# Longer operand tiles: four buffers of a tag begin at four different places of a 128-byte line

## The chip, the cores and the metric

The kernel runs on one NeuronCore of a Trainium2 chip. The metric is the device time of one execution in microseconds (us); the median of several runs counts. TensorE, VectorE (DVE), ScalarE (ACT), GpSimd (POOL) and SyncE (SP) run their own queues and meet at semaphores. SBUF has 128 partitions; a tile occupies the same bytes of every partition.

## The reference

Two decoder layers over 256 tokens of 2048 features, all in float32:

```
x += NSA(rmsnorm(x));       x += square(relu(rmsnorm(x) @ w_up)) @ w_down     (layer 0)
k, v = rmsnorm(x) @ w_kv                                                      (shared, once)
x += DiffAttn(rmsnorm(x));  x += square(relu(rmsnorm(x) @ w_up)) @ w_down     (layer 1)
return rmsnorm(x)
```

NSA has 16 query heads and 4 key heads of 128. It has three branches: keys and values compressed from blocks of 32 tokens by a small MLP, selected blocks, and a window. With 256 tokens all blocks are selected and the window covers everything. DiffAttn takes the difference of two softmaxes for each of 16 heads. The hidden width of the MLPs is 8192, so the four MLP weights are most of the 390 MB that are read.

## The kernel before, in words

**Split products.** TensorE multiplies a reduced form of float32 (fp32r). To keep the precision, each operand is split into a high part (`split`, L144: a copy on ScalarE that rounds) and a low part (a subtraction on VectorE), and a product is three matmuls: high by high, high by low, low by high (`mm3`, L139). All of these are issued at L132.

**The weight stream.** `plan` lists 368 units of 512 x 512 weights in the order of use. `issue_raw` (L253) loads a unit as two halves into `raw` tiles, `issue_split` (L265) splits each half into a tile `wh` and a tile `wl` of 128 x 1024. Loads run up to four units ahead of use, splits two. Each of the tags `raw`, `wh`, `wl` has four buffers, so that two units of split weights are on the chip.

**The products.** There are three kinds, by what is stationary in the array and what streams through it (the moving operand):
- `unit_mm` (L291) in `proj` and `out_proj`: stationary are 128 x 128 pieces of activations in a `big` tile, moving are 512 columns of `wh` or `wl`. One unit is 24 matmuls, 12 on each half.
- `unit_mm` in the MLP's down projections: the same, but the activations lie in a `kv` tile.
- `up_unit` (L704): the weights are stationary (128 columns of `wh` or `wl`), the activations in `big` are moving: 512 columns (high and low parts side by side) with `wh`, then 256 columns (high part) with `wl`, in turn. One unit is 16 pairs.

The MLP goes through four groups (G) of 2048 hidden units: four chunks of up projections (64 pairs each), then 16 units of down projections. In the compression (`cmp_units`, L506) the stationary operand is `X[j][:, l, :]`, 120 columns or 480 bytes for each l, in a `big` tile; moving are `wh` and `wl`.

**The order.** TensorE's order is written out: the stream of units runs on, and generators for the attention heads, transposes and so on are resumed between its steps (`tick`, L107). The queues of TensorE and SyncE keep this order; the other engines' instructions are ordered by the framework.

**Where tiles lie.** `T` (L70) takes a tile of a tag from the pool; a tag has a fixed number of buffers (`BUFS`, L66), which its tiles take in turn. The tags lie one behind the other in each partition, the buffers of a tag one behind the other. A buffer of `big` has 16384 bytes, of `wh` and `wl` 4096, of `kv` 8192; these are multiples of 128, so all four buffers of a tag begin at the same place within 128 bytes. From the sizes of all that lies before them, `big` begins 64 bytes past a multiple of 128, and `wh`, `wl` and `kv` 96. The query tiles `qth` and `qtl` begin at 96 too.

Of the kernel before, what the change touches and what calls it, by code (L numbers as in the profile page):

```python
# [20 lines left out]
EPS = 1e-6  # L21
NEG = -3.0e38
FLOOR = -1.0e38
# NSA heads: waits before the scores, the transposes and the values; head to head; first head
WAIT_A = (2.0, 12.5, 4.0, 1.5, 7.0)
# differential heads: the same, and before the normed output's transposes
WAIT_B = (1.0, 8.5, 5.0, 5.5, 9.0, 7.0)
LAMBDA_INIT = 0.8 - 0.6 * math.exp(-0.3 * 1)

# [2 lines left out]
def kernel(  # L32
# [24 lines left out]
    sb = ctx.enter_context(tc.tile_pool(name="sb", bufs=2))  # L57
# [4 lines left out]
    def name(s):  # L62
        uid[0] += 1
        return f"{s}_{uid[0]}"

    BUFS = dict(raw=4, wh=4, wl=4, big=4, kv=4, q=3, qth=2, qtl=2, sa=2, sbt=2,  # L66
                psh=1, psl=1, pwh=1, pwl=1,
                ss=2, rs=2, rb=1, nrs=1, mx=3, den=3, sq=2)

    def T(shape, tag, dt=F32):  # L70
        return sb.tile(shape, dt, tag=tag, name=name(tag), bufs=BUFS[tag])

    PB = dict(acc=4, tp=4)

    def PT(tag):
        return pp.tile([P, 512], F32, tag=tag, name=name(tag), bufs=PB[tag])

# [1 line left out]
    # The weight products run as a steady stream; the pieces that wait on other  # L79
    # engines are generators, resumed between the stream's steps once the time  # L80
    # that they asked for has gone by on the tensor engine's own count.
    clock = [0.0]
    tasks = []
    seq = [0]
# [22 lines left out]
    def tick():  # L107
        if tasks and tasks[0][0] <= clock[0]:
            step()
# [21 lines left out]
    def mm(o, l, r, start, stop, shared=False):  # L131
        nc.tensor.matmul(o, lhsT=l, rhs=r, start=start, stop=stop, skip_group_check=shared)  # L132
        clock[0] += max(o.shape[-1], 256) / 2400.0

    def transpose(o, i, idn):
        nc.tensor.transpose(o, i, idn)  # L136
        clock[0] += 0.11
# [6 lines left out]
    def split(h, l, src, scale=None):  # L144
        if scale is None:
            nc.scalar.activation(h, src, AF.Copy)  # L146
            nc.vector.tensor_tensor(l, src, h.bitcast(F32), ALU.subtract)  # L147
        else:
            nc.scalar.activation(h, src, AF.Copy, scale=scale)
            nc.vector.scalar_tensor_tensor(l, src, scale, h.bitcast(F32), ALU.mult, ALU.subtract)  # L150

    ctx.enter_context(tc.manual_schedule(engines={mybir.EngineType.PE, mybir.EngineType.SP}))

# [1 line left out]
    cst = cp.tile([P, 640], F32, name="cst")  # L155
    ident = cst[:, 0:128]
    cmask = cst[:, 128:384]
# [20 lines left out]
    gates = cp.tile([P, 2, 48], F32, name="gates")  # L178
# [14 lines left out]
    def g_kv(k):  # L193
        return gcol2[:, 32 + k:33 + k]

# [1 line left out]
    plan = []  # L197

    def add_units(w, rows, c0):
# [12 lines left out]
        add_units(win, range(4), c * 512)  # L212

    def out_order():
        # (column chunk, head group): the later a group's heads come out, the later its part
        return ([(0, 0), (1, 0), (0, 1), (1, 1), (2, 0), (2, 1), (3, 0), (3, 1)] + [(2, 2), (3, 2), (0, 2), (1, 2)]
                + [(c, 3) for c in range(4)])

# [3 lines left out]
    for c, g in out_order():  # L222
        add_units(nsa_w_out[0], [g], c * 512)

    def down_order(last):
        # (column chunk, quarter of the group's rows); at the very end the last quarters of two
        # chunks stay on chip and are used for one token tile after the other
        if not last:
            return [(c, u) for c in range(4) for u in range(4)]
        return ([(c, u) for c in range(2) for u in range(4)] + [(c, u) for c in (2, 3) for u in range(3)]  # L230
                + [(2, 3), (3, 3)])
# [13 lines left out]
    for c, g in out_order():  # L245
        add_units(diff_w_out[0], [g], c * 512)
# [3 lines left out]
    units = {}  # L250
# [47 lines left out]
                    start and kk == 0, stop and kk == 3)  # L298
                tick()

# [1 line left out]
    def new_stats():  # L302
        return T([P, 2, 4], "ss"), T([P, 2], "rs")

# [28 lines left out]
                          tp[:, kk * 256:(kk + 1) * 256], gf(k))  # L333

    def new_xt():
        # two tiles of eight feature blocks: [feature, block, part, token]
        return [T([P, 8, 2, S], "big", F32R) for _ in range(2)]

    def rope(dst, src, n, rot, ct, stb):
# [17 lines left out]
        return o  # L357

    def transpose_k(src, th, tl):
        # th, tl: [dk, kv head, token block, token]  # L360
        for pr in range(2):
            if pr:
                yield 0.8
            tp = PT("tp")
            for hh in range(2):
                for t in range(2):
                    h = pr * 2 + hh
                    transpose(tp[:, hh * 256 + t * P:hh * 256 + (t + 1) * P],
                              src[:, t, h * P:(h + 1) * P], ident)
            hs = slice(2 * pr, 2 * pr + 2)  # L370
            split(th[:, hs], tl[:, hs], tp.rearrange("p (h t q) -> p h t q", h=2, t=2))
# [5 lines left out]
    def new_kv(*shape):  # L377
        return T([P, *shape], "kv", F32R)


# [1 line left out]
    with tc.high_priority():  # L382
        for c in range(4):
            if c == 0:
# [16 lines left out]
        nc.vector.tensor_scalar(gsub, gcol2[:, 48:49], 1.0 - LAMBDA_INIT, None, ALU.mult)  # L401
        yield 0.0

    # =========================== layer 0: NSA ===========================
    ss, rs = new_stats()
    xt = new_xt()
    xts = [spawn(xt_chunk(c, [(lambda k: g_attn(0, k), xt)]), 5.5 * c - 2.0) for c in range(4)]
# [58 lines left out]
        X.append(T([P, 32, 120], "big", F32R))  # L466
        tX.append(spawn(make_X(tok, X[j], j)))

    # gates: the stationary operand holds both parts of the weights side by side
    gwp = [T([P, 8, 96], tag, F32R) for tag in ("wh", "wl")]  # L470
    for i in range(2):
        split(gwp[i][:, :, 0:48], gwp[i][:, :, 48:96], gw[:, 8 * i:8 * i + 8, :])
# [89 lines left out]
    half = cp.tile([P, 1], F32, name="half")  # L562
# [139 lines left out]
        return done  # L702

    def up_unit(us, ps, xt, k0):  # L704
        # weights stationary: the product comes out with the hidden units on partitions, the
        # part with the high half of the activations and the one with the low half side by side
        for pair in range(2):
            for kk in range(4):
                wh, wl = us[kk // 2]
                k = k0 + kk  # L710
                both = xt[k // 8][:, k % 8].rearrange("p s q -> p (s q)")
                for b in (2 * pair, 2 * pair + 1):
                    bs = slice(b * P, (b + 1) * P)
                    mm(ps[b], wh[:, kk % 2, bs], both, k == 0, False)
                    mm(ps[b][:, 0:S], wl[:, kk % 2, bs], both[:, 0:S], False, k == 15)
                tick()
# [75 lines left out]
    mlp(0, mxt, rs2, hook0, done)  # L792
    finish_stats(ssd, rsd)

    # =========================== layer 1: differential attention ===========================
    lamt = T([P, 256], "sbt")
    nc.gpsimd.dma_start(lamt, diff_lambda.rearrange("b f d -> b (f d)").to_broadcast([P, 256]))
    lv = lamt.rearrange("p (a b d) -> p a b d", a=2, b=2)
# [10 lines left out]
    ps = proj(kxt, before=xts)  # L809
    t_ = evac_tok(ps, rsd)  # L810
    rope(t_, t_, 8, 16, cosB, sinB)
    # keys of the two components side by side, each with zeros on the other's rows:
    # [.., kv head, (first tile: c0, c1; second tile: c0, c1), key]
    dkh, dkl, dv = new_kv(4, 4, P), new_kv(4, 4, P), new_kv(2, 4, 2, P)
    for d in (dkh, dkl):
        for cc in range(2):
# [19 lines left out]
    ready = [spawn(diff_keys(), 6.0)]  # L836
    ps = proj(kxt)
    for t in range(2):
        # [key, key tile, kv head, part, value column]
        split(dv[:, t, :, 0, :], dv[:, t, :, 1, :], ps[t].rearrange("p (g d) -> p g d", g=4), rsd[:, t:t + 1])  # L840

    oth, otl = T([P, 16, 256], "big", F32R), T([P, 16, 256], "big", F32R)
# [2 lines left out]
    def diff_head(hd, qr):  # L845
        g, i = hd // 4, hd % 4
# [44 lines left out]
        yield WAIT_B[2]  # L891
        yield from s_o.take()
        o = PT("tp")
        # columns: (first tile: main, low part of the values; second tile: the same)
        for t, blocks in ((0, ((0, 0),)), (1, ((1, 0), (2, 1)))):
            for n, (s_, kt) in enumerate(blocks):
                a = slice(s_ * P, (s_ + 1) * P)
# [68 lines left out]


def _consts():
    """Identity, causal masks and rotary tables: they depend on the shapes alone."""
    import numpy as np  # L970

    c = np.zeros((128, 640), np.float32)
    p = np.arange(128)
    c[:, 0:128] = np.eye(128, dtype=np.float32)
    c[:, 256:384] = np.where(p[None, :] <= p[:, None], 0.0, NEG)
    n = np.arange(32)
    for t in range(2):
        ok = (n[None, :] < 15) & (16 * n[None, :] + 31 <= (t * 128 + p)[:, None])
        c[:, 384 + 32 * t:416 + 32 * t] = np.where(ok, 0.0, NEG)

    def tables(head_dim, o):
        rot = head_dim // 4
        h = rot // 2
        e = (np.arange(0, rot, 2, dtype=np.float32) / np.float32(rot)).astype(np.float32)
        inv = (np.float32(1.0) / np.power(np.float32(500000.0), e)).astype(np.float32)
        ang = np.arange(S, dtype=np.float32)[:, None] * inv[None, :]
        cos, sin = np.cos(ang).astype(np.float32), np.sin(ang).astype(np.float32)
        for t in range(2):
            r = slice(t * 128, (t + 1) * 128)
            c[:, o + t * rot:o + t * rot + h] = cos[r]  # L990
            c[:, o + t * rot + h:o + (t + 1) * rot] = cos[r]
            b = o + 2 * rot + t * rot
            c[:, b:b + h] = -sin[r]
            c[:, b + h:b + rot] = sin[r]

    tables(128, 448)
    tables(64, 576)
    return c
# [24 lines left out]
```

## Time and profile before

| | |
|---|---|
| median of 3 runs | 2161.58 us (2161.39 to 2163.61) |
| profiled execution: span from its first to its last instruction | 2159.3 us |
| profiled execution: its own time | not recorded apart from the span; the median of the runs is 2.3 us above the span |
| mean granted TensorE clock | 0.999 |
| read from HBM | 390.47 MB, 182 GB/s over the span |

[...] What a matmul costs the stream is the time from its start to the start of the next, and that is got from a stretch's length and its count of matmuls.

### The profile page before, as it was taken

The page shows a single profiled execution, that of the slowest core. Times are in us where ns is not written, and L with a number is a line of the kernel's source. Part 1 is how long each engine was busy: PE and PEld are TensorE (multiplying, and loading weights), DVE is VectorE, ACT ScalarE, POOL GpSimd, SP SyncE. Part 2 cuts the span into 40 slices and gives each one's busy share as a digit, 9 for nine tenths or more (in the row PEclk, how much of TensorE's full clock was granted, in tenths as well). Part 3 has the DMA queues.
Part 4 walks back from the last instruction along what each step waited for, and adds up shares of the span by engine and source line. Part 5 has one row for each costly group of instructions (what it writes and reads, how often), then busy time and mean ns, then how long its engine had stood idle before and what let it go on. Part 6 is the DMA issues. An engine that isn't in the chain of part 4 may idle for free.

```text
span 2159.3 us, 28803 instructions
## 1 busy us (share of the span) xinstructions
PE 2135.1 (99%) x10780; PEld 1794.7 (83%) x10780; DVE 1333.7 (62%) x2156; ACT 1082.7 (50%) x1737; POOL 81.4 (4%) x121
## 2 busy tenths in 40 slices
PE   8999999999999999999999999999999999999998
PEld 6877888888888888888888877888888888888886
DVE  5665777666546656555666578866656655655654
ACT  6665666454434434434555466664434434544443
POOL 0111100000000000000000111000000000000000
PEclk9999999999999999999999999999999999999999
DMA  7787432455566566666655543356566556566654
GB/s 244 238 266 242 124 100 90 145 171 184 196 194 189 193 194 186 195 195 188 188 191 185 185 146 127 127 186 188 193 194 186 195 194 187 187 199 190 192 193 142
DMA packets 204828, 394.45 MB, mean 183 GB/s; under 512 B 14176, under 2 KB 14368, under 8 KB 204560
## 3 DMA queue, kind: packets, MB, share of 16 engines
q1 hardware_dynamic: 203936, 390.51, 57.2%
q0 software_dynamic: 560, 2.02, 0.3%
q8 instruction: 84, 1.38, 0.3%
q14 instruction: 56, 0.46, 0.1%
q10 hardware_dynamic: 192, 0.08, 0.0%
HBM read 390.47 MB, written 2.10 MB: 182 GB/s over the span
## 4 chain that ended last, share of the span: by engine, by line
PE 94%; DVE 2%; ACT 1%; DMA 1%; issue 1%; POOL 0%; SPq 0%; DVEq 0%; POOLq 0%; ACTq 0%
PE acc L132 59%; PE tp L132 33%; PE tp L136 2%; DVE wl L147 1%; DMA raw<-in_nsa_w_in_dram 1%; ACT wh L146 1%; DMA raw<-in_nsa_cmp_w_dram 0%; ACT sa L874 0%; ACT sbt L874 0%; POOL sq L910 0%; DVE psl L147 0%; DVE big L150 0%; DVE sbt L881 0%; DVE pwl L906 0%; DVE pwl L912 0%
## 5 line engine op out<-in xcount | busy, mean ns | idle before, releaser
L147 DVE TENSOR_TENSOR wl<-raw,wh 128x1024 fp32r<-128x1024 f32 x736 | 902.4, 1228 | 711.9 <-ACT wh L146 705.4
L146 ACT ACTIVATE wh<-raw 128x1024 fp32r<-128x1024 f32 x736 | 777.8, 1058 | 825.4 <-PE acc L132 489.3
L132 PE MATMUL acc<-wh,big 128*128 128x512 f32 (+1 forms) x1600 | 548.0, 403 | 1.3 <-ACT wh L146 1.3
L132 PE MATMUL acc<-wh,kv 128*128 128x512 f32 x1280 | 397.2, 390 | 0.0
L132 PE MATMUL tp<-big,wh 128*128 128x512 f32 (+1 forms) x1040 | 359.5, 392 | 0.0
L132 PE MATMUL acc<-big,wh 128*128 128x512 f32 x1024 | 357.9, 394 | 0.0
L132 PEld LDWEIGHTS acc<-wh,big 128*128 128x128 f32 (+1 forms) x1600 | 300.9, 188 | 67.4 <-ACT wh L146 1.7
L132 PE MATMUL acc<-wl,big 128*128 128x512 f32 (+1 forms) x832 | 329.1, 396 | 0.5 <-DVE wl L147 0.5
L132 PE MATMUL tp<-big,wl 128*128 128x256 f32 (+1 forms) x1040 | 288.9, 280 | 0.0
L132 PE MATMUL acc<-big,wl 128*128 128x256 f32 x1024 | 286.8, 280 | 0.0
L132 PEld LDWEIGHTS acc<-wh,kv 128*128 128x128 f32 x1280 | 240.3, 188 | 50.1
L132 PE MATMUL acc<-wl,kv 128*128 128x512 f32 x640 | 249.0, 389 | 0.0
L132 PE MATMUL tp<-wh,kv 128*128 128x512 f32 x768 | 237.4, 389 | 0.0
L132 PEld LDWEIGHTS tp<-big,wh 128*128 128x128 f32 (+1 forms) x1040 | 194.3, 187 | 44.0
L132 PEld LDWEIGHTS acc<-big,wh 128*128 128x128 f32 x1024 | 192.3, 188 | 43.6
L132 PEld LDWEIGHTS tp<-big,wl 128*128 128x128 f32 (+1 forms) x1040 | 194.9, 188 | 0.0
L132 PEld LDWEIGHTS acc<-big,wl 128*128 128x128 f32 x1024 | 192.9, 188 | 0.2
L132 PEld LDWEIGHTS acc<-wl,big 128*128 128x128 f32 (+1 forms) x832 | 156.7, 188 | 31.3 <-DVE wl L147 1.0
L132 PEld LDWEIGHTS tp<-wh,kv 128*128 128x128 f32 x768 | 144.2, 188 | 29.9
L132 PE MATMUL tp<-wl,kv 128*128 128x512 f32 x384 | 149.4, 389 | 0.0
L132 PEld LDWEIGHTS acc<-wl,kv 128*128 128x128 f32 x640 | 120.2, 188 | 24.4
L146 ACT ACTIVATE kv<-q 128x256 fp32r<-128x256 f32 x128 | 50.0, 412 | 73.4 <-DVE q L735 73.4
(183 smaller groups left out, 1416.7 us busy)
## 6 DMA issues: line engine op xcount, KB each, us to landing
raw<-in_mlp_w_up_dram SPq DMA_DIRECT2D x256, 512.0 KB, 3.9
raw<-in_mlp_w_down_dram SPq DMA_DIRECT2D x256, 512.0 KB, 4.3
raw<-in_nsa_w_in_dram SPq DMA_DIRECT2D x80, 512.0 KB, 4.4
raw<-in_nsa_cmp_w_dram SPq DMA_DIRECT2D x32, 512.0 KB, 4.8
raw<-in_nsa_w_out_dram SPq DMA_DIRECT2D x32, 512.0 KB, 3.7
raw<-in_diff_w_q_dram SPq DMA_DIRECT2D x32, 512.0 KB, 3.7
raw<-in_diff_w_out_dram SPq DMA_DIRECT2D x32, 512.0 KB, 3.7
raw<-in_kv_w_shared_dram SPq DMA_DIRECT2D x16, 512.0 KB, 3.5
```

The lines of the kernel that those rows point to most:

```text
L132: nc.tensor.matmul(o, lhsT=l, rhs=r, start=start, stop=stop, skip_group_check=shared)
L136: nc.tensor.transpose(o, i, idn)
L146: nc.scalar.activation(h, src, AF.Copy)
L147: nc.vector.tensor_tensor(l, src, h.bitcast(F32), ALU.subtract)
```

## The change

Tiles of the tags `big`, `wh`, `wl` and `kv` are allocated with 8 more float32 elements, 32 bytes, in each partition, and a view of the old size is cut from the front. The four buffers of such a tag then begin at 0, 32, 64 and 96 bytes past the place of its first one, modulo 128. Four times 32 is 128, so that the tags behind a staggered one begin at the same place within 128 bytes as before. All users take the same slices of the view. Comments are dropped elsewhere in the file; `raw` and the other tags stay as they were. The tiles grow by 16 x 32 = 512 bytes in each partition altogether.

```
+    STAGGERED = ("big", "wh", "wl", "kv")
+
     def T(shape, tag, dt=F32):
-        return sb.tile(shape, dt, tag=tag, name=name(tag), bufs=BUFS[tag])
+        if tag not in STAGGERED:
+            return sb.tile(shape, dt, tag=tag, name=name(tag), bufs=BUFS[tag])
+        n = math.prod(shape[1:])
+        flat = sb.tile([shape[0], n + 8], dt, tag=tag, name=name(tag), bufs=BUFS[tag])[:, 0:n]
+        if len(shape) == 2:
+            return flat
+        dims = [f"d{i}" for i in range(1, len(shape))]
+        return flat.rearrange(f"p ({' '.join(dims)}) -> p {' '.join(dims)}", **dict(zip(dims, shape[1:])))
```

## Rows read from the trace of the kernel before

**Rows 1.** The page: busy time of each engine, and the granted clock in 40 slices.
```profile
span 2159.3 us, 28803 instructions
PE 2135.1 (99%) x10780; PEld 1794.7 (83%) x10780; DVE 1333.7 (62%) x2156; ACT 1082.7 (50%) x1737; POOL 81.4 (4%) x121
...
PEclk9999999999999999999999999999999999999999
```

**Rows 2.** The page: the chain that ended last, shares of the span.
```profile
PE 94%; DVE 2%; ACT 1%; DMA 1%; issue 1%; POOL 0%; SPq 0%; DVEq 0%; POOLq 0%; ACTq 0%
PE acc L132 59%; PE tp L132 33%; PE tp L136 2%; DVE wl L147 1%; DMA raw<-in_nsa_w_in_dram 1%; ACT wh L146 1%; DMA raw<-in_nsa_cmp_w_dram 0%; ACT sa L874 0%; ACT sbt L874 0%; POOL sq L910 0%; DVE psl L147 0%; DVE big L150 0%; DVE sbt L881 0%; DVE pwl L906 0%; DVE pwl L912 0%
```

**Rows 3.** TensorE's waits: who waited for whom, total us, times, longest.
```profile
PE tp L136 <- DMA cst<-in_consts_dram: 5.8, 1, 5.8
PE tp L136 <- DVE pwl L912: 1.9, 3, 1.2
PE tp L136 <- ACT sa L520: 1.4, 2, 0.8
PE acc L132 <- ACT wh L146: 1.3, 1, 1.3
...
PE acc L132 <- DVE wl L147: 0.5, 1, 0.5
```

**Rows 4.** The chain in order of time: start us, us, what, instructions merged.
```profile
481.13 22.61 PE tp L132 x128
...
636.06 22.19 PE acc L132 x128
...
768.37 43.52 PE tp L132 x192
...
1198.93 44.80 PE acc L132 x192
...
1467.40 22.61 PE tp L132 x128
...
2040.54 22.19 PE tp L132 x128
```

**Rows 5.** The page's costliest groups: TensorE's matmuls, busy us, mean ns, idle before.
```profile
L132 PE MATMUL acc<-wh,big 128*128 128x512 f32 (+1 forms) x1600 | 548.0, 403 | 1.3 <-ACT wh L146 1.3
L132 PE MATMUL acc<-wh,kv 128*128 128x512 f32 x1280 | 397.2, 390 | 0.0
L132 PE MATMUL tp<-big,wh 128*128 128x512 f32 (+1 forms) x1040 | 359.5, 392 | 0.0
L132 PE MATMUL acc<-big,wh 128*128 128x512 f32 x1024 | 357.9, 394 | 0.0
...
L132 PE MATMUL acc<-wl,big 128*128 128x512 f32 (+1 forms) x832 | 329.1, 396 | 0.5 <-DVE wl L147 0.5
...
L132 PE MATMUL acc<-wl,kv 128*128 128x512 f32 x640 | 249.0, 389 | 0.0
L132 PE MATMUL tp<-wh,kv 128*128 128x512 f32 x768 | 237.4, 389 | 0.0
...
L132 PE MATMUL tp<-wl,kv 128*128 128x512 f32 x384 | 149.4, 389 | 0.0
```

**Rows 6.** Timeline of TensorE at a head's scores: start us, us, what, count.
```profile
256.00 0.40 PE L132 MATMUL acc<-wh,big 128*128 128x512 f32 x1
256.24 0.40 PE L132 MATMUL acc<-wl,big 128*128 128x512 f32 x1
256.47 0.39 PE L132 MATMUL acc<-wh,big 128*128 128x512 f32 x1
256.70 0.62 PE L132 MATMUL tp<-kv,qth 128*128 128x512 f32 x2
257.16 0.39 PE L132 MATMUL tp<-kv,qtl 128*128 128x512 f32 x1
257.38 0.40 PE L132 MATMUL tp<-kv,qth 128*128 128x256 f32 x2
```

**Rows 7.** Timeline of TensorE in the compression (120 stationary columns).
```profile
71.06 0.39 PE L132 MATMUL acc<-wl,big 128*120 128x512 f32 x1
...
72.45 0.39 PE L132 MATMUL acc<-wl,big 128*120 128x512 f32 x1
72.68 0.40 PE L132 MATMUL acc<-wh,big 128*128 128x512 f32 x1
```

**Rows 8.** The page's costliest groups: the splits of the weights.
```profile
L147 DVE TENSOR_TENSOR wl<-raw,wh 128x1024 fp32r<-128x1024 f32 x736 | 902.4, 1228 | 711.9 <-ACT wh L146 705.4
L146 ACT ACTIVATE wh<-raw 128x1024 fp32r<-128x1024 f32 x736 | 777.8, 1058 | 825.4 <-PE acc L132 489.3
```

## The prediction

> **What bounds the kernel now.** [...] So the end moves only with the time from one matmul's start to the next (the pitch), or if another engine becomes late. Next the waits: of TensorE's own, those for split weights are 1.3 and 0.5 us [rows 3]; the stream is not short of operands.
>
> Then the chain in order of time, which cuts the stream into stretches with a count, so that a pitch can be divided out [rows 4]:
> - Down projections (moving `wh`/`wl`, stationary `kv`): 43.52 us for 192 matmuls, 226.7 ns each.
> - Up projections (moving `big`, stationary `wh` or `wl`, 512 and 256 columns in turn): 22.19 us for 128 matmuls, 346.7 ns a pair, in the groups after the first. In the first group of each layer the same code on the same tiles takes 22.61, 353.3 ns a pair. The chain has 24 stretches of the first kind; 8 chunks are of the slow one.
> - Projections with moving `wh`/`wl` and stationary `big`: 44.80 us for 192, 233.3 ns each.
>
> [...]
>
> What differs between the stretches is where the two operands begin. While a matmul streams, the weights of the next one are loaded. I call the gap the place of the moving operand less that of the next stationary one, modulo 128 bytes. Before, `big` begins 64 past a multiple of 128 and `wh`, `wl`, `kv` 96, and every slice taken of them except the compression's is a multiple of 128. So the gap is 0 in the down projections (226.7), 32 in the other projections (233.3), 96 in the up projections (346.7 or 353.3). Two rows test this. In a head, keys (`kv`) stream against queries (`qth`, also at 96): gap 0; three such matmuls start between 256.70 and 257.38, 226.7 ns each, straight after projections with 240 and 230 [rows 6]. The compression steps through its stationary operand by 480 bytes, so that it meets all four gaps in turn, two matmuls each: 71.06 to 72.68 us for seven, 231.4 each [rows 7]. And the two kinds of up stretch say that the gap is not all: with one and the same gap the stream runs in a fast or a slow rhythm, fast where it came out of gap 0, slow where it came out of gap 32.
>
> **The change part by part.** No instruction, wait, DMA or queue entry is added, removed or moved: the same slices are taken of tiles 32 bytes longer. The price can only lie in pitches, or in the time of the splits.
>
> *The splits.* ScalarE takes 1058 and VectorE 1228 ns for one [rows 8]; TensorE works 12 x 226.7 = 2720 ns on each pair. Were a split to become a fifth longer, it would still fit more than once on its engine beside the other work (62% and 50%), so I cost it at nothing. If that cover were gone, 736 splits x 1.2 us x 0.2 = 177 us of VectorE time would have somewhere to show, beside 38% of 2159 = 820 us of idle time.
>
> *The new gaps.* Buffer k of a staggered tag begins 32k bytes further on than before, modulo 128. Counting the program's matmuls by the buffer that each tile gets in turn gives, for gaps 0 / 32 / 64 / 96: down 737 / 1145 / 752 / 437; projections and compressions 617 / 702 / 605 / 508; up pairs 512 of each.
>
> Prices for a 512-column matmul: gap 0, 226.7; gap 32, 233.3; gap 96 is seen only in the alternating rhythm, which is as cheap as gap 0 (13.3 ns a matmul over its columns) or 3.3 dearer, so bounds 226.7 and 233.3, and I take the middle, 230. Gap 64 no long stretch shows. [...] I take 231.4, the compression's, the nearest row that has this gap in it.
> - Down, against 226.7: 1145 x 6.6 = +7.6; 437 x 3.3 = +1.4; 752 x 4.7 = +3.5. Sum +12.5 us.
> - Projections, against 233.3: 617 x 6.6 = -4.1; 508 x 3.3 = -1.7; 605 x 1.9 = -1.1. Sum -6.9 us.
> - Up: 512 pairs are slow now. If gaps 0 and 96 run fast and 32 and 64 slow, 1024 will be: 512 x 6.6 = +3.4 us. Bounds: all fast -3.4, all slow 1536 x 6.6 = +10.1.
> - At each change of buffer (two in a unit of weights, 736 in all) the stream jumps 32 bytes, 8 columns or 3.3 ns to either side: -2.5 to +2.5 us, taken as 0.
>
> Together +9.0 us. The profiled execution spans 2159.3 us; the median of the runs is 2161.6, so 2.3 us lie around the span, where nothing changes. Forecast: 2161.6 + 9.0 = 2170.6 us. The reason in a sentence: the stages that fill most of the time stand in the best gap or rhythm that the trace shows, and the change gives each stage the average.
>
> [...] The trace's matmuls differ by 6.6 ns with operand and stretch, at one clock and without a wait [rows 3, 4]. [...]
>
> **The rivals.**
> 1. *The gaps count modulo 64 and cancel.* Then 64 is as good as 0 and 96 as bad as 32. For: nothing in the rows tells the two readings apart. Against: gap 96 runs fast in 24 of 32 up chunks. Down (1145 + 437) x 6.6 = +10.4, projections -(617 + 605) x 6.6 = -8.1, up -3.4 to +3.4: -1.1 to +5.7, middle 2163.9 us.
> 2. *Faster: at gap 64 the two reads miss each other.* A mechanism of its own: if the loss comes from both reads meeting in the same part of a 128-byte line, half a line apart would be the place where they don't. [...] Against: the compression passes it and averages 231.4 [rows 7]. [...] It decides from small sums on: the other terms make +9.0 - 5.8 = +3.2 us, and 752 + 605 + 1024 matmuls at gap 64 pay that back at 1.3 ns each. [...]
> 3. *The place of an operand changes nothing,* and the three pitches come from something else that differs between the stretches (tile shapes, PSUM tags): 2161.6 us. For: the two rhythms of one gap. Against: the head's matmuls, which fall to 226.7 at once.
>
> **How the numbers follow.** What a measurement of this kernel tells from no change is about 0.2%, 4.3 us. Chances: the forecast 0.45, its own range 2165 to 2192 (all up slow, and the 512-column ones at up to 233.3: 3072 x 6.6 + 10.1 = +30.4 us is its end); the cancelling case 0.18, of which 0.11 is within 0.2% and 0.07 slower; the faster one 0.32; no effect 0.05. Of the forecast I put 0.04 within 0.2%. So faster 0.32, same 0.20, slower 0.48. The range for 8 in 10 takes in the forecast's but for its last end and the faster case down to 2140: 2140 to 2190.
>
> **What would show it.** In the chain in order of time the down stretches of 192 matmuls would take some 44.3 us instead of 43.52 (12.5 us over 16 such), the projections 44.3 instead of 44.80, the up stretches of later groups between 22.2 and 22.6. Inside a unit the pitch would step every 12 matmuls with the buffer: that is the gap at work; an even pitch through the unit would be rival 3. If down stretches fall under 43.5, gap 64 is cheap and rival 2 holds. Waits of TensorE for `wh` or `wl` above the 1.8 us of now would show that the splits were not covered. My prediction is wrong where the pitch at gap 64 lies well under 226.7, or where a mixed stream finds a rhythm that the pure ones don't have.

## The result and the profile after

The changed kernel takes **2178.39 us** (median of 4 runs, 2176.34 to 2179.61), the kernel before in the same series 2161.48 (2161.29 to 2163.61). The ratio is 1.0077, interval 1.0064 to 1.0089: slower by some 17 us. The forecast was 2170.6, slower by 9.0. The profiled execution spans 16.4 us more.

The page of the kernel after: the span, busy time of each engine, shares of the chain that ended last, and the groups of the splits ([rows 1, 2, 8] are the same lines of before).

```profile
span 2175.7 us, 28804 instructions
PE 2151.2 (99%) x10780; PEld 1796.8 (83%) x10780; DVE 1334.8 (61%) x2156; ACT 1083.1 (50%) x1737; POOL 81.3 (4%) x121
...
PE 92%; DVE 3%; DMA 2%; ACT 1%; issue 1%; POOL 0%; SPq 0%; DVEq 0%; POOLq 0%; ACTq 0%
...
L157 DVE TENSOR_TENSOR wl<-raw,wh 128x1024 fp32r<-128x1024 f32 x736 | 903.3, 1229 | 726.6 <-ACT wh L156 719.3
L156 ACT ACTIVATE wh<-raw 128x1024 fp32r<-128x1024 f32 x736 | 778.3, 1059 | 840.9 <-PE acc L142 489.7
```

The counts of matmuls and splits are the same. TensorE is busy 16.1 us longer, nearly the whole loss, and a split takes 1229 and 1059 ns where it took 1228 and 1058. TensorE's waits for split weights, the last two below, were 1.3 and 0.5 us [rows 3]: no new wait for them. Those for `sa` and `big`, 1.4 and 0.7 before, grew a little (us in total, times, longest).

```profile
PE tp L146 <- ACT sa L530: 2.0, 2, 1.5
...
PE tp L142 <- DVE big L160: 1.7, 2, 0.9
...
PE acc L142 <- ACT wh L156: 0.9, 1, 0.9
...
PE acc L142 <- DVE wl L157: 0.5, 1, 0.5
```

So the stream itself is slower. The chain of the kernel after in order of time (start us, us, what, instructions merged) answers to [rows 4]:

```profile
479.75 22.41 PE tp L142 x128
...
635.94 22.42 PE acc L142 x128
...
725.57 44.52 PE acc L142 x192
770.09 44.45 PE tp L142 x192
...
1206.74 44.50 PE acc L142 x192
...
2054.89 22.39 PE tp L142 x128
```

- Down: 192 matmuls take 44.45 to 44.52 us instead of 43.52. Sixteen such stretches lose 16 x 0.95 = some 15.2 us.
- Up: 22.39 to 22.42 in every group. The 24 chunks that took 22.19 lose some 24 x 0.21 = 5.1, the 8 that took 22.61 win 8 x 0.21 = 1.7: together +3.4.
- Projections: 44.50 for 44.80 in the full stretches; on the path the attention parts win 1.4 us (layer 0) and 0.6 (layer 1) between them, found from the start times of the same matmul in both traces. The same comparison gives +9.2 us for each MLP. Over the 1955 projection matmuls that nothing interrupts the mean pitch fell from 233.1 to 231.7 ns.

15.2 + 3.4 - 2.0 = 16.6 us, against 16.4 measured.

One surprise stood in the timeline of TensorE (start us, us, what, count): in a down unit of the kernel after whose weights and activations lie at gap 0 modulo 128, as those of all down units of before do, the pitch is not 226.7.

```profile
787.04 0.63 PE L142 MATMUL tp<-wh,kv 128*128 128x512 f32 x2
...
787.74 0.63 PE L142 MATMUL tp<-wh,kv 128*128 128x512 f32 x2
...
788.44 0.63 PE L142 MATMUL tp<-wh,kv 128*128 128x512 f32 x2
```

A product of three starts every 0.70 us, 233 ns a matmul. The 732 down matmuls at gap 0 that nothing interrupts average 231.6, those at 32, 64 and 96 232.1, 230.5 and 232.8. The gap modulo 128 hardly orders them.

### The profile page after: what moved, and what is told of

Read it like the earlier page. It is cut to its first block, busy times and chain, and to the rows that moved or that the text cites. A ratio compares the mean times of both kernels' runs of the same rounds, so it can differ in the third digit from the quotient of the medians.

```text
span 2175.7 us, 28804 instructions
## 1 busy us (share of the span) xinstructions
PE 2151.2 (99%) x10780; PEld 1796.8 (83%) x10780; DVE 1334.8 (61%) x2156; ACT 1083.1 (50%) x1737; POOL 81.3 (4%) x121
## 4 chain that ended last, share of the span: by engine, by line
PE 92%; DVE 3%; DMA 2%; ACT 1%; issue 1%; POOL 0%; SPq 0%; DVEq 0%; POOLq 0%; ACTq 0%
PE acc L142 58%; PE tp L142 33%; PE tp L146 2%; DMA raw<-in_nsa_cmp_w_dram 1%; DVE wl L157 1%; ACT wh L156 1%; DMA raw<-in_nsa_w_in_dram 1%; ACT sbt L884 0%; ACT sa L884 0%; POOL sq L920 0%; DVE sbt L891 0%; DVE big L160 0%; DVE psl L157 0%; DVE sa L891 0%; DVE pwl L916 0%
## 5 line engine op out<-in xcount | busy, mean ns | idle before, releaser
L157 DVE TENSOR_TENSOR wl<-raw,wh 128x1024 fp32r<-128x1024 f32 x736 | 903.3, 1229 | 726.6 <-ACT wh L156 719.3
L156 ACT ACTIVATE wh<-raw 128x1024 fp32r<-128x1024 f32 x736 | 778.3, 1059 | 840.9 <-PE acc L142 489.7
L142 PE MATMUL acc<-wh,kv 128*128 128x512 f32 x1280 | 402.7, 394 | 0.0
```

## Experiments

All experiments were timed against the kernel before on the same chip, which took 2161.9 to 2162.6 us. In each, `T` is that of the change with two tables in place of its fixed 8: `EXTRA`, by how many floats (4 bytes) a tile is longer, and `LEAD`, how many floats its view begins later. Tags that stand in neither are as before. The edit against before, for e1 (`T` goes on as in the change):

```
+    LEAD = dict(big=8)
+    EXTRA = dict(big=32)
     def T(shape, tag, dt=F32):
-        return sb.tile(shape, dt, tag=tag, name=name(tag), bufs=BUFS[tag])
+        if tag not in EXTRA:
+            return sb.tile(shape, dt, tag=tag, name=name(tag), bufs=BUFS[tag])
+        n, o = math.prod(shape[1:]), LEAD.get(tag, 0)
+        flat = sb.tile([shape[0], n + EXTRA[tag]], dt, tag=tag, ...)[:, o:o + n]
         ...
```

Where nothing else is said, a fence holds stretches of the chain in order of time, of 192 matmuls (down where the tile is `tp`, projections where it is `acc`) and of 128 (up). Means by gap are worked out from the starts in the trace and the places that the built program gives each tile, over matmuls that nothing interrupts. The buffers of a tag do not come in strict turn, which is why the gaps are unequally frequent (437 to 1145 of the down matmuls).

**First round: one gap for a whole kernel.** Are the prices those of the gap modulo 128, and does the mixing cost?

*e1_all96*, the tables above: `big` goes to 96, so that down, projections and up all stand at gap 0.

> No stagger; only big begins 32 bytes later, at 96 like wh, wl and kv, so that the gap (place of the moving operand less that of the next stationary one, modulo 128) is 0 in every unit of the stream except the compression. Gap theory (the pitch of a matmul follows from its own gap): projections fall from 44.80 us for 192 to 43.5, the first up group from 22.61 to 22.2, total 2161.5 - 16 - 3 = about 2142 us. Steadiness theory (what costs is that the places change every 12 matmuls; a stream with unchanging places settles into a rhythm, and gap 0 has the cheap one): the same 2142. Rival (the pitches belong to the kind of product, and places do not matter): 2161.5, projections still at 44.8.

Measured 2165.01 us, ratio 1.0013 (1.0003 to 1.0023): a miss by 23 us.

```profile
479.67 22.53 PE tp L143 x128
...
768.01 43.52 PE tp L143 x192
...
1200.56 44.34 PE acc L143 x192
```

Down is untouched, but the projections win little and the up projections lose (22.47 still at 2043 us). The tile's 128 extra bytes, nothing modulo 128, had put its buffers 128 bytes apart modulo 256. In the projection stretch TensorE's timeline shows both places, first a `big` tile at gap 0 modulo 256, then, from 1214 us on, one 128 bytes off:

```profile
1203.39 0.39 PE L143 MATMUL acc<-wl,big 128*128 128x512 f32 x1
...
1205.43 0.39 PE L143 MATMUL acc<-wl,big 128*128 128x512 f32 x1
...
1214.29 0.40 PE L143 MATMUL acc<-wl,big 128*128 128x512 f32 x1
...
1217.77 0.39 PE L143 MATMUL acc<-wl,big 128*128 128x512 f32 x1
```

Nine matmuls from 1203.39 to 1205.43 take 226.7 ns each, fifteen from 1214.29 to 1217.77 take 232.0. That became the theory of the second round. The place is not all, however: right behind a head's transposes, from 1200.63 to 1202.71, nine matmuls in place took 231. And for the up projections the same place is not the cheap one: the half chunks at gap 0 modulo 256 take 353.1 ns a pair, those 128 off 351.

*e2_all0*: `LEAD` big 16, wh, wl, kv 8; `EXTRA` 32 for all four. Everything at 0 modulo 128, and so at gap 0.

> No stagger; big, wh, wl and kv all begin at a multiple of 128: gap 0 everywhere, at place 0 instead of 96. Gap and steadiness theories: as all at 96, about 2142 us. Rival (the absolute place counts: at place 0 the kernel after the change has gap-0 matmuls at 235, 235, 230 ns): down projections 44.8 us for 192, up 22.6 for 128, total about 2161.5 + 20 + 10 = 2190 us.

2177.73 us, 1.0071 (1.0056 to 1.0086): neither the 2142 of the two theories nor the 2190 of the rival. With gap 0 modulo 128 everywhere, all of the change's loss is there; the projections take 44.19. Modulo 256 the buffers again lie 128 bytes apart. That the absolute place counts is refuted by the same trace: the 16 half units (12 matmuls) of down projections at place 0 that follow another half unit in place run at 226.7 ns throughout, as at place 96 before.

```profile
657.85 22.47 PE tp L143 x128
...
769.56 44.32 PE tp L143 x192
```

*e3_gap64*: `LEAD` big 24, kv 16; `EXTRA` big 32, kv 32. Gap 64 modulo 128 everywhere.

> No stagger; wh and wl at 96, big and kv at 32: the gap is 64 in every unit except the compression. Gap theory with the prices read in the kernel after the change (gap 64: 230.5 down, 231.3 in the up stream): down 44.3 us for 192, total about 2161.5 + 12 - 6 + 0 = 2167 us. Reading modulo 64 (64 is as good as 0): about 2142 us. Steadiness theory: any unchanging gap settles, to a rhythm of its own that is between 226.7 and 233.3: 2142 to 2190.

2187.42 us, 1.0117 (1.0102 to 1.0133): 20 us above what the prices by gap gave.

```profile
660.16 22.61 PE tp L143 x128
...
772.58 44.59 PE tp L143 x192
```

Up takes 22.61 in every group and the projections 44.81: half of 128 bytes apart is no shelter. Modulo 256 the gap is 64 or 192 here, by the buffer; down takes 231.4 ns at the one and 233.3 at the other. A gap of 64 modulo 256 throughout was not run.

*e4_step64*: `EXTRA` 16 for all four, no lead. Buffers step by 64 bytes, so that modulo 64 nothing moves.

> The tiles are 64 bytes longer instead of 32, so that the four buffers begin at 0, 64, 0, 64 past the first one's place. Places modulo 64 are those of the kernel before, but places modulo 128 change every 12 matmuls. If places count modulo 64: 2161.5 us and down stretches of 43.52. If they count modulo 128 and a change costs, as the steadiness theory has it: like the kernel after the change, 2172 to 2180 us, down stretches of 44.2 to 44.6.

2175.84 us, 1.0063 (1.0048 to 1.0078); down 44.15 and 44.35. Rival 1, a period of 64, is refuted.

**Second round: which period, and what of it counts.** Only `kv` is longer, by 128, 256 or 512 bytes; weights and projections stay as before.

*e5_kv128*: `EXTRA` kv 32.

> Only the kv tiles are 128 bytes longer; the places of all tiles modulo 128 are those of the kernel before, but the four buffers of kv now differ by 128 modulo 512, so that the gap in the down projections (moving wh or wl, next stationary kv) is 0, 128, 256 or 384 modulo 512 in turn. If the gap counts modulo 128: 2161.5 us, down stretches of 43.52. Theory now held (the cheap rhythm of the down projections needs a gap of 0 modulo a longer period, 256 or 512 bytes): down stretches of about 44.4 us, as in the kernel with all at 0, 16 stretches x 0.9 = +14 us, total about 2175.

2176.40 us, 1.0070 (1.0055 to 1.0085).

```profile
659.89 22.61 PE tp L143 x128
...
771.88 44.10 PE tp L143 x192
...
1208.62 44.81 PE acc L143 x192
...
1655.48 22.19 PE tp L143 x128
```

Inside the down stretch, in the timeline of TensorE, the pitch follows the buffer of `kv`:

```profile
785.91 0.61 PE L143 MATMUL tp<-wh,kv 128*128 128x512 f32 x2
...
787.95 0.64 PE L143 MATMUL tp<-wh,kv 128*128 128x512 f32 x2
...
791.43 0.64 PE L143 MATMUL tp<-wh,kv 128*128 128x512 f32 x2
```

Nine matmuls from 785.91 to 787.95 take 226.7 each, with `kv` at a multiple of 256 from the weights; then `kv` is 128 off, and fifteen to 791.43 take 232.0 each. Over all such units it is 227.3 and 232.7. Where a unit in place follows one out of place (44 units), the first three matmuls average 229.9, the next three 227.2 and 227.0, and only then comes 226.7: here the cheap rhythm has to be run into. And the up stretches, whose operands all lie as before, run at 22.61 through all of layer 0, and at 22.19 in the later groups of layer 1. The 24 down matmuls ahead of those groups run at 232.9 ns in layer 0 and at 227.1 to 227.2 in layer 1: the slower down projections hand their cost on.

*e6_kv256*: `EXTRA` kv 64. *e7_kv512*: `EXTRA` kv 128.

> Only the kv tiles are 256 bytes longer: the gap in the down projections is 0 or 256 modulo 512. Period 256 (or 128): 2161.5 us, down stretches of 43.52. Period 512: units at gap 256 leave the cheap rhythm, down stretches of 43.8 to 44.3, total 2166 to 2174.

> Only the kv tiles are 512 bytes longer: the gap stays 0 modulo 512. Theory with a period of up to 512: 2161.5 us, down stretches of 43.52. If the stretch of 8192 bytes from buffer to buffer is what counts (a longer period, or the length itself): about 44.4 and 2175, as with 128 bytes.

2163.34 us, 1.0005 (0.9995 to 1.0014), and 2162.13 us, 1.0001 (0.9992 to 1.0010): nothing. The stretches of e6 are those of [rows 4], and e7 has the same:

```profile
659.30 22.19 PE tp L143 x128
...
769.42 43.52 PE tp L143 x192
```

Longer tiles cost nothing by themselves, and the period for the down projections is 256 bytes: steps of 64 (e4, 2175.84 us) and 128 (e5, 2176.40) cost, 256 (e6, 2163.34) does not.

**Third round: what in the change does it, and what a place can win.**

*e8_placed*: `LEAD` big 8, `EXTRA` big 128 (512 bytes, a multiple of 256). Projections stand at gap 0 modulo 256; the MLP's activations keep their old place:

```
-    def new_xt():
+    def new_xt(lead=None):
-        return [T([P, 8, 2, S], "big", F32R) for _ in range(2)]
+        return [T([P, 8, 2, S], "big", F32R, lead) for _ in range(2)]
...
-                box["xt"] = new_xt()
+                box["xt"] = new_xt(0)
```

> No stagger. The big tiles are 512 bytes longer, which keeps the places of their four buffers alike modulo 512; where they are stationary (all projections, compression) they begin 32 bytes later, at gap 0 modulo 512 with wh and wl; the MLP's transposed activations, which are moving in the up projections, stay where they were before. Theory of a period of 256 or 512: projections fall from 44.80 us for 192 to 43.5 (2304 matmuls x 6.6 ns = -15 us), the first up group, entered from the cheap rhythm, from 22.61 to 22.19 (-3 us), down as before; total about 2143 us, faster than both. If instead no arrangement of big helps (the projections' pitch is of their kind): 2161.5.

2156.02 us, 0.9973 (0.9962 to 0.9983): faster than before, by 13 us less than expected.

```profile
479.64 22.61 PE tp L143 x128
...
656.76 22.19 PE tp L143 x128
...
766.87 43.52 PE tp L143 x192
...
1196.69 43.58 PE acc L143 x192
```

The full projection stretches fall from 44.80 to 43.58 as the theory wants. Two parts of the forecast failed. The first up group of each layer stays at 22.61: fast projections before it don't help. Transposes and norms lie between, which is the likely reason and was not tested.

And of the projections' gain a part was not kept. Over 2015 matmuls the mean fell from 233.1 to 228.3 (9.7 us), but the kernel's median fell by 6.5, and the profiled execution, the slowest of the eight, spans only 3.1 less than that of before. Its trace shows where. TensorE waits 4.0 us for `sa`, the compressed sums that ScalarE reads out of PSUM, where it waited 1.4 [rows 3]. It starts the last matmul ahead of the first of the two waits 1.6 us earlier, but `sa` comes no earlier: the chain that leads to it holds weight loads of 5.34 us from 113.01 and 5.56 us from 120.80, with a split of 1.24 between them, where the kernel before has TensorE's matmuls on it from 104.26 to 124.09. TensorE's timeline before, then in e8 (in brackets the wait):

```profile
128.72 0.63 PE L136 MATMUL tp<-cst,sa 120*128 120x120 f32 x4 [0.68 <-ACT sa L520]
```

```profile
128.63 0.63 PE L147 MATMUL tp<-cst,sa 120*128 120x120 f32 x4 [2.18 <-ACT sa L531]
```

Soon after this wait of 2.18 us the granted clock fell from 1.00 to 0.50, for 3.4 us from 130.0 on, and it did so once more at 1341.8, behind a run of waits of which the last is 1.20 us long. (Before has nearly the same waits at that place and no such fall.) A stretch of e8 (us, then busy us and instructions of PE, PEld, DVE, ACT and POOL, granted clock, DMA share, GB/s):

```profile
131.00:132.00 1.00, 1.00 (x4) 0.81 (x3) 1.00 (x2) 0.06 (x1) 0.82 (x1) 0.50 1.00 367
```

A matmul takes 427 ns there, so each such stretch costs some 1.6 us (an estimate: 3.4 us at 427 instead of 227 ns). The profiled executions of e2, e6, e9, e10 and e11 have one of them, near 1350 us; the others, before and the change among them, have none. So a difference of 1 to 2 us between the attention parts of two traces need not come from the layout.

*e9_wl128*: `LEAD` wl 32, `EXTRA` wl 64. Every buffer keeps its place modulo 128, none alternates; only `wl` lies 128 off `wh` modulo 256, as after the change, where `wh`'s four buffers (4 x 4128 bytes) push it there.

> No stagger; nothing moves modulo 128. Only the wl tiles begin 128 bytes later modulo 256 than wh (their four buffers alike), so that within every product of three matmuls (wh, wl, wh) the gap alternates between 0 and 128 modulo 256 in the down projections. Theory (the cheap rhythm needs a gap that is 0 modulo 256 and stays so for some ten matmuls; staggering by 32 bytes also put wl 128 bytes off wh modulo 256): the down stretches lose it, 44.3 to 44.6 us instead of 43.52, 16 x 0.9 = +14 us or more, up stretches not at 22.19 throughout, total 2174 to 2182. Rival (the loss after the change comes from the 32-byte steps): 2161.5.

2180.39 us, 1.0081 (1.0064 to 1.0098).

```profile
659.09 22.44 PE tp L143 x128
...
770.79 44.37 PE tp L143 x192
...
1207.77 44.81 PE acc L143 x192
```

This one displacement costs as much as the whole change. In down the matmuls at gap 0 take 232.2 ns and those at gap 128 take 229.9: in this stream gap 0 brings nothing. So a matmul's pitch is no function of its own gap alone.

*e10_kv_only*: `EXTRA` kv 8. *e11_w_only*: `EXTRA` wh 8, wl 8. The two halves of the change for the down projections.

> The change's stagger on kv alone. Its four buffers begin at 0, 32, 64, 96 past the first, so only one unit in four of the down projections has gap 0 modulo 256 (24 matmuls at a time). Theory: down stretches about 0.25 x 43.6 + 0.75 x 44.5 = 44.3 us, +12 us, up to +4 where the up rhythm is then entered slow; projections 44.80 as before; total 2172 to 2178. Rival (kv has no part in it): 2161.5.

> The change's stagger on wh and wl alone. The gap changes with every half unit and, wl lying 128 off wh modulo 256, also inside each product of three. Theory: all three kinds as after the change: down 44.4 to 44.6, up 22.4, projections 44.4 to 44.8 us; total about 2176 to 2180, that is, the weights alone do all that the change does.

e10 takes 2188.25 us, 1.0119 (1.0104 to 1.0134), worse than the whole change; e11 2178.50, 1.0073 (1.0058 to 1.0088), the same as the whole. The stretches of e10, then of e11:

```profile
661.07 22.61 PE tp L143 x128
...
773.46 44.57 PE tp L143 x192
```

```profile
659.61 22.39 PE tp L143 x128
...
771.23 44.45 PE tp L143 x192
...
1207.62 44.52 PE acc L143 x192
```

The projections of e10 take 44.81, as before. e11's stretches are those of the change to within 0.07 us: longer `wh` and `wl` are enough for all of it. The two halves do not add: longer `kv` alone costs 25.9 us, and together with the others the whole costs 16.9. Longer `big` alone was not run. In e10 a unit at gap 0 falls to 226.7 after some ten matmuls, and those at 160, 192 and 224 stay at 233 to 234. Its up projections lost some 10 us, where at most 4 were expected: the operands lie as before, but all chunks are entered in the slow rhythm, as in layer 0 of e5.

*e12_placed_up32*: as e8, but the MLP's activations (moving in up) lie 32 bytes *above* the weights' place and not 32 below.

```
-                box["xt"] = new_xt(0)
+                box["xt"] = new_xt(16)
```

> As the kernel with placed activations, but the MLP's moving activations begin 64 bytes later, at gap +32 instead of -32 to the weights. If the up rhythm depends on the size of the gap alone: up stretches 22.19 or 22.61 as before, total 2156. If it depends on which operand is ahead: one of them throughout, 22.61 in all groups (+10 us, 2166) or 22.19 in all (-3 us, 2153).

2149.61 us (2148.67 to 2150.43), 0.9940 (0.9926 to 0.9955): the fastest of all, 0.6% below before.

```profile
476.67 22.19 PE tp L143 x128
...
652.49 22.19 PE tp L143 x128
...
762.58 43.52 PE tp L143 x192
...
1192.37 43.58 PE acc L143 x192
```

The first group runs at 22.19 now, worth 8 x 0.42 = 3.4 us. The profiled execution spans 7.5 us less than that of e8; most of the rest is the two stretches at a clock of 0.50, 2 x 1.6 us by the estimate above, which it does not have. Its page's span and chain shares:

```profile
span 2148.7 us, 28803 instructions
...
PE 91%; DVE 3%; DMA 3%; ACT 2%; issue 1%; POOL 0%; SPq 0%; POOLq 0%; DVEq 0%; ACTq 0%
```

DMA's share of the chain went from 1% [rows 2] to 3%. The slower kernel after has 2%, so the share alone does not show a new bound; TensorE's wait for `sa`, 2.9 us where it was 1.4, is the place where the faster stream comes too early.

## Why the prediction was right or wrong

The way was right, and the size about half: 9.0 of 16.9 us.

**The bound** held. TensorE, busy 99% at a granted clock of 0.999 and 94% of the chain before [rows 1, 2], stays busy 99% after, at 0.999. The end moved with the pitch of the matmuls and with little else: busy time +16.1, span +16.4 us.

**The splits** at nothing: right, they kept their durations and TensorE's waits for them did not grow.

**That the place of the operands sets the pitch** (against rival 3): shown. e5 and e7 differ only in the length of `kv`, and by 14 us. The row that the prediction held against this rival, three head matmuls at 226.7 [rows 6], was a favourable one: over the 23 such threes of that trace that nothing interrupts the mean is 229.1 ns, single matmuls 224 to 236.

**Where the sum failed** is the step "gap 0, 226.7", with the prices by the gap modulo 128. Two things replace it. The period is 256 bytes (e5 against e6), which the kernel before could not tell, since all its buffers are multiples of 256. And the pitch belongs to the run as much as to the matmul. With all operands in place it takes some six to twelve matmuls to settle at 226.7 (e1, e4, e5, e10). With every third matmul 128 bytes off, the same two places cost differently by what went before: half units of down projections with `wh` at gap 0 and `wl` at 128 average 231.3 ns in e9 and 229.0 in e11, and in the kernel after 230.0 where the half unit before stood at gap 160 and 233.3 where it stood at 32 or 224. Nowhere do they run at 226.7 throughout. After the change both conditions of the cheap rhythm are gone: `wl` lies 128 off `wh`, and the place changes every 12 matmuls. Either alone costs about as much: e9 has only the first (18.0 us slower), e4 only the second, in steps of 64 bytes (14.0). So the 737 down matmuls counted as free cost 5 ns each. Term by term, of the 7.9 us that the forecast lacks:
- Down: +12.5 forecast, some +15.2 measured. The gap-0 matmuls add 737 x 5.0 = 3.7 us; the other gaps at their measured means (232.1, 230.5, 232.8) come out 0.8 us lower together.
- Projections: -6.9 forecast, -2.0 on the path, at 4.9 us the largest error. Their 617 matmuls at gap 0 run at 230.5 and not at 226.7, for the same reason, and the 44.50 of a full stretch gives only 0.7% where 3% would be the price of gap 0. The mean pitch fell by 1.4 ns, 3.2 us over 2304 matmuls. The other 1.2 is about what waits took that the sum had left out: those for `sa` and for `big` grew from 1.4 and 0.7 to 2.0 and 1.7 us, that for `wh` fell by 0.4.
- Up: +3.4 forecast and +3.4 measured, right by luck. I counted half of the chunks fast and half slow; in fact all run at one middle pitch, 22.39 to 22.42.
- Buffer jumps: 0 forecast. They were not priced by themselves; the settling suggests that what they cost is the rhythm behind them.

No run shows two terms of the sum: the 13.3 ns a matmul over its columns, by which gap 96 counted as cheap as gap 0, and the 3.3 ns for 8 columns at a change of buffer. In their place the runs showed 232.8 ns for the down matmuls at gap 96 after the change, where the sum had 230, and 229.9 ns for the first three matmuls back in place behind a change of buffer (e5). The shortest time from the start of a 512-column matmul to the next start is 224 ns in the traces of before and after.

"The pitch would step every 12 matmuls with the buffer" was so only where the rest of the layout is still: in e5 it steps with `kv`'s buffer (226.7, then 232.0). In the kernel after it hardly does: 230.5 to 232.8 at all gaps. The closing warning, a mixed stream with a rhythm of its own, is what came.

**Rival 1** fell with e4 (2175.84 where its period of 64 gives no change). **Rival 2** fell with e3 (2187.42, down at 231.4 ns at gap 64): no long stretch under 226.7 ns was seen at any gap. Yet the faster side was there, by another way than I had written: not gap 64, but the old good gap for the projections too, and 32 above for up: e12 with 2149.61.

**What the place alone costs.** `kv` 128 bytes longer, with no instruction and no wait changed, takes the half of the down matmuls that come to lie 128 off from 226.7 to 232.7 ns, and 256 bytes longer costs nothing (e5, 2176.40 us; e6, 2163.34). By what mechanism the two places act on the pitch, no run here can say.

## What to carry to other kernels

Where TensorE is busy 99% and waits for nobody, divide the chain's stretches by their counts: unequal pitches at one clock and one shape can be a layout's price, here 6.6 of 233.3 ns. For this kernel's streams of 512 columns throughout, the cheap layout has the moving operand and the stationary one at the same place modulo 256 bytes (projections 43.58 us for 192 in e8, 44.80 before), all buffers of a tag and both halves of a split operand alike: with `kv`'s buffers 128 bytes apart (e5) it took 2176.40 us, with `wl` 128 off `wh` (e9) 2180.39, against some 2162 before. For the alternating up stream that is not the best place: 346.7 ns a pair with the moving operand 32 bytes above (e12), 353.1 (e1) and 350.8 (e2) in half chunks at the same place. A pad of 256 or 512 bytes cost nothing here (2163.34 and 2162.13 us, e6 and e7); shorter ones of `kv` cost (32 bytes, e10: 2188.25; 128, e5: 2176.40), and a pad can move every tag behind it (`wl` by `wh`'s pad: e11, 2178.50). Then look whether the gain was kept: in e8 and e12 the faster stream reached `sa` before it was there, and waited 4.0 and 2.9 us for it where it had been 1.4.

## What the runs showed of the hardware that was not expected

- *Two rhythms at one layout.* With the moving operand 32 bytes below the next stationary one, the alternating up stream of 512 and 256 columns runs at 22.19 or 22.61 us per 128, and keeps the one in which it is entered: in e5 all of layer 0 at 22.61, then in layer 1 the later groups at 22.19, with the same places. With the operand 32 bytes above (e12) only 22.19 to 22.21 was seen, even behind the transposes; with buffers alternating between gap 0 and 128 modulo 256 (e1) it is 22.45 to 22.53. Why the sign counts is open, and +32 was tried once.
- *What one matmul's gap says.* In e11's down projections the means by gap modulo 256 are 226.8 at 0, 233.0 at 32, 230.7 at 64, 234.9 at 96, 233.5 at 128, 235.0 at 160, 229.9 at 192 and 231.6 at 224; in e9 gap 0 has 232.2 and gap 128 229.9. The neighbours, and what ran before them, count as much as the matmul itself, and a table of prices by gap, as I had made it, does not carry over from one layout to another.
